# A two-layer decoder trunk on one core: sparse-attention probabilities times values as split products for four heads at once, more projections by halves of K, and a raw-weight ring of three

## The chip, the core and the metric

The kernel runs on one core of a Trainium2 chip. The core has five engines with queues of their own: TensorE (PE, with its weight loads shown as PEld), VectorE (DVE), ScalarE (ACT), GpSimd (POOL) and SyncE (SP, which issues the transfers). The metric is the device time of one execution in microseconds (us), the median of several runs. Every time below is from the profile of one execution or from those runs.

## What is computed

A sequence of 512 tokens of width 1024 goes through two layers. Each layer normalises, projects, runs two groups of attention heads, multiplies each branch by a gate, projects back and adds; after that comes a gated per-layer embedding. The change touches mostly branch A of layer 0, a sparse attention in which each query keeps its best 128 causal keys by an indexer's score. Eight query heads share one key and one value head of 64 columns:

```python
def _dsa_attention(q, k, v, q_idx, k_idx, w_idx):      # cut
    ...
    score = jnp.where(causal[None], score, -jnp.inf)
    _, sel = lax.top_k(score, top_k)
    ...
    kg = k[bidx, sel]
    vg = v[bidx, sel]
    s = jnp.einsum('bqhd,bqkd->bqhk', qb, kg) * scale
    pr = jax.nn.softmax(s, axis=-1).astype(v.dtype)
    return jnp.einsum('bqhk,bqkd->bqhd', pr, vg)

def _even_layer(...):                                  # cut
    oa = _dsa_attention(aq, ak, av, iq, ik, iw)
    ob = _sliding_window_sink_attention(bq, bk, bv, b_sinks)
    ya = oa.reshape(bsz, seq, A_WIDTH) * jax.nn.silu(ag)
    yb = ob.reshape(bsz, seq, B_WIDTH) * jax.nn.silu(bg)
    return jnp.concatenate([ya, yb], axis=-1) @ w_out
```

Layer 1 has the branches C (dilated attention) and D (differential attention) in the same frame.

## The kernel before

Tokens are worked in four tiles of 128 (`NT`), the model width in eight pieces of 128 (`NK`). A product that has to be exact to float32 is made of split operands: `hilo` (line 337) writes a value's rounded part with ScalarE (`hi`) and the remainder with VectorE (`lo`), both in the reduced float32 format, and `PASSES` (line 381) multiplies hi by hi, hi by lo and lo by hi, three matmuls of 512 columns. Weights come in through `load_w` (line 346) into a ring of four tiles `raw` of 128x512, are split into a ring of eight tiles `w2`, and are multiplied by the split activations `AT`.

`proj_tok` (line 388) has three orders. "kt" runs over the K pieces outside and the four output banks `mm` inside, so that all four banks are complete at the end; "mix" does the first four K pieces so, and then, one bank after the other, the last four, handing each bank over as it is complete; "tok" does one bank after the other. `proj_gate` (line 443) makes a branch's gate and has one order, that of "kt".

Attention of A and B is `attend_four` (line 693): for one query tile `qb` and four heads, scores into the banks `sk`, then `exp_rows` (VectorE adds the mask and takes the row's extreme, ScalarE exponentiates), ScalarE scales by the reciprocal of the sum, and `probs_t` (line 633) turns the probabilities by TensorE transposes into the one bank `tk`, which ScalarE copies to `pt` in float32. Then one float32 matmul of 128 columns for each head and key block multiplies `pt` by the values `Ve` into the bank `ob`, and `put_y` writes the result to `Y`, by ScalarE, or by VectorE with the gate multiplied in where the gate is there already. C already does it the other way: `turned` (line 623) transposes up to four blocks, `hilo` splits them into `pt`, and matmuls with up to 512 columns multiply them by a value tile whose 128 columns are 64 of hi and 64 of lo; `add_halves` adds the two halves of the result.

The order of the instructions of all engines is not the order of the code. `Program` records every call, and `order` (line 211) lays them out by a list schedule: on each engine the ready call of lowest rank goes first, where a rank is the call's place in the code less a lead from the table `LEADS` (line 31). The orders are then fixed; each engine works its list from front to back. SyncE issues all weight loads and the moves of heads. All is in one function, and the trace gives every instruction the line of its outer caller (L260), so that the rows below are told apart by tile names.

Of the kernel before, what the change touches and what calls it, by code (L numbers as in the profile page):

```python
# [12 lines left out]
F32 = mybir.dt.float32  # L13
# [8 lines left out]
P = 128  # L22
# [9 lines left out]
    "att": (-47, 57, 0, 53, 0, 124, 103, 328, -453, -409, 0, 0, 65, 346, 15, -135, -12, -62, 201, 25, 64, -25, -77,  # L32
# [6 lines left out]
    "idx": (-5, 38, 12),  # L39
    "mm": (0, 71, -13, 0, 0, 8, -171, 58, -43, 0, 16, 1, 0, 0, -20, 0, -21, 212, 58, -17, 0, 42, 10, -107, 178, -10,  # L40
         -7, -2, 8, -2),
    "norm": (-1359, -2, 2, 0, 228, -8, -7, -723, -109, 136, 0, 728, -122, -190, 196, 14, 146, 1654, 86, -1, 1, 0,
         -277, -9),
    "rows": (-312, -61, 0, -98),
    "rs": (0, 0, 160),
    "ss": (121, 0, -149, -59, -2, 107, -255, -64, 1, 167, 231, 226, 0, -95, 298, 72, 0, 34, 18, 45, -118, -139, -39,
         0, -102, 85, 7, 30, -79, -161, 0, -49),
    "tab": (2592, 1756, 76, 2, -41, 0),
    "top": (0, -183, -691, -1133, 45, 7, 5, 0, 5, -296, -294, -351),
    "w": (0, 226, 357, 520, 348, 94, -40, 291, 8, -115, 15, 22, 54, -173, 0, 41, 45, 193, -113, -15, 99, 144, -123,  # L50
         59, 194, -22, -64, -41, -621, -1474),
    "x": (-445, -66),
    "y": (1366, 84, 36, 1, 1288, 252, 91, -16, 10, 0, 1032, 24, -46, -55, -384, -1003),
    None: 0,
# [5 lines left out]
PR = 8  # L60
SHORT = 400
# [202 lines left out]
def tile_trunk(ctx: ExitStack, tc: tile.TileContext, a: dict, out: bass.AP):  # L264
# [9 lines left out]
    def uid(s):  # L274
        cnt[0] += 1
        return f"{s}{cnt[0]}"
# [10 lines left out]
    def o_bank():  # L287
        return ps.tile([P, 512], F32, name=uid("ob"), tag="ob", bufs=1)
# [57 lines left out]
    def load_w(parts, kts):  # L346
        raws = []
        n = sum(w for _, w in parts)
        for kt in kts:
            raw = sb.tile([P, 512], F32, name=uid("raw"), tag="raw", bufs=4)  # L350
            o = 0
            for src, w in parts:
                nc.sync.dma_start(out=raw[:, o:o + w], in_=src[kt * P:(kt + 1) * P, :])
                o += w
            raws.append((kt, raw[:, :n]))
        return raws, n
# [86 lines left out]
    def proj_gate(pieces_n, y0, done, rsb, swap=0):  # L443
# [3 lines left out]
        for i, (kt, w2) in enumerate(pieces):  # L447
            for m in range(4):
                for c, (xa, wa) in enumerate(PASSES):
                    nc.tensor.matmul(banks[m], w2[:, wa, m * P:(m + 1) * P], AT[:, xa, kt ^ (4 * swap), :],  # L450
                                     start=(i == 0 and c == 0), stop=(i == last and c == 2))
# [241 lines left out]
    def attend_four(qb, key0, qT, kv, g, V, mask, y0, sink=None):  # L693
# [130 lines left out]
    for k0, k1 in ((1, 2), (2, 3), (3, 4)):  # L824
        load_xT(k0, k1)
        wiq[0].extend(load_w(ecols("iq"), range(k0, k1))[0])
# [116 lines left out]
    proj_tok(wbq, head_evac(bqT, (tab_bq[:, 0], tab_bq[:, 1]), rs0, put=put_stacked))  # L943
# [5 lines left out]
    proj_tok(waq, head_evac(aqT, (tab_aq[:, 0], tab_aq[:, 1]), rs0, put=put_stacked))  # L949
# [55 lines left out]
    proj_tok(weights(ocols("cv"), range(NK), 2), cv_evac, swap=1)  # L1005
# [83 lines left out]
    proj_tok(wcq, head_evac(cqT, (tab_cq[:, 0], tab_cq[:, 1]), rs1, put=put_far), swap=1)  # L1089
# [5 lines left out]
    proj_tok(weights(ocols("dv"), range(NK), 2), dv_evac, swap=1)  # L1095
# [4 lines left out]
    proj_tok(wdk, head_evac(dkT, (tab_dk[:, 0], tab_dk[:, 1]), rs1, put=put_stacked), swap=1)  # L1100
    wdq = weights(ocols("dq"), range(NK), 2)
    dqT = {}
    proj_tok(wdq, head_evac(dqT, (tab_dq[:, 0], tab_dq[:, 1]), rs1, put=put_far), swap=1)
# [68 lines left out]
```

## Time and profile before

| | us |
|---|---|
| median of three runs | 664.13 (663.04 to 664.13) |
| the profiled execution | 663.99 |
| its span, from first to last instruction | 662.1 |
| TensorE busy | 655.2 |
| VectorE busy | 531.9 |
| ScalarE busy | 415.9 |

The span is 1.9 us shorter than the time of the same execution; the rest lies around it. The page gives each engine's busy time, the span in 40 slices of 16.6 us with a digit for each (tenths of the slice that the engine was busy), the chain of work that ended last, and groups of instructions by tile. A busy TensorE means that matmuls are in its pipe, not that it starts one at every chance; how fast they follow each other is read from how many fit in a stretch.

### The profile page before, as it was taken

How to read it: one execution, taken by the hardware profiler on the slowest of the kernel's cores; microseconds unless marked ns; L12 is line 12 of the kernel's file. 1: busy time of each engine (PE TensorE's matmuls, PEld its weight loads, DVE VectorE, ACT ScalarE, POOL GpSimd, SP SyncE). 2: the span in 40 equal slices, each digit the busy share in tenths (PEclk: the TensorE clock that was granted, in tenths of full speed). 3: DMA queues.
4: the chain of work that ended last, by engine and by line, in shares of the span. 5: the costliest groups of instructions: out<-in, count | busy, mean ns of one | idle time of the engine just before them, and what ended most of it. 6: DMA issues, size and time to landing. Idle time of an engine off the chain costs nothing.

```text
span 662.1 us, 10348 instructions
## 1 busy us (share of the span) xinstructions
PE 655.2 (99%) x3373; PEld 542.4 (82%) x3373; DVE 531.9 (80%) x1246; ACT 415.9 (63%) x937; POOL 66.3 (10%) x46
## 2 busy tenths in 40 slices
PE   9999999999999999999999999999999999999997
PEld 5888788889888888888878888888887878888886
DVE  6798999999999656786796297788697899768565
ACT  6675659989799933654564254776654586655431
POOL 0121133010000000000031041000053100000000
PEclk9999999999999999999999999999999999999999
DMA  8945155546111530542545438621286672323411
GB/s 329 341 134 144 49 147 156 160 132 219 33 57 43 189 96 16 175 144 94 161 141 148 125 120 257 196 81 49 74 244 175 213 224 66 121 61 98 127 65 64
DMA packets 76711, 90.50 MB, mean 137 GB/s; under 512 B 6640, under 2 KB 43888, under 8 KB 76400
## 3 DMA queue, kind: packets, MB, share of 16 engines
q1 hardware_dynamic: 76512, 89.81, 44.5%
q8 instruction: 27, 0.44, 0.3%
q14 instruction: 28, 0.23, 0.1%
q10 hardware_dynamic: 144, 0.02, 0.0%
HBM read 69.36 MB, written 10.49 MB: 121 GB/s over the span
## 4 chain that ended last, share of the span: by engine, by line
PE 90%; DMA 4%; DVE 3%; SPq 1%; issue 1%; ACT 1%; POOL 0%; POOLq 0%
PE mm L260 69%; PE ob L260 8%; PE tk L260 7%; PE sk L260 7%; DMA far<-ql 2%; DVE t L260 1%; SPq L260 1%; DMA raw<-in_w_in_odd_dram 1%; DMA raw<-in_w_in_even_dram 1%; DMA slot<-far 1%; DVE w L260 1%; DVE tiny L260 1%; DMA q<-far 0%; POOL tiny L260 0%; ACT w L260 0%
## 5 line engine op out<-in xcount | busy, mean ns | idle before, releaser
L260 PE MATMUL mm<-AT,w 128*128 128x512 f32 (+1 forms) x1176 | 293.9, 394 | 0.0
L260 PEld LDWEIGHTS mm<-AT,w 128*128 128x128 f32 x1176 | 211.6, 188 | 40.0 <-ACT raww L260 0.3
L260 PE MATMUL mm<-w,AT 128*128 128x512 f32 (+1 forms) x936 | 237.8, 398 | 0.3 <-DVE w L260 0.2
L260 PEld LDWEIGHTS mm<-w,AT 128*128 128x128 f32 x936 | 170.7, 188 | 34.8 <-DVE w L260 0.5
L260 ACT ACTIVATE w<-raw,gains 128x512 fp32r<-128x512 f32 x96 | 67.8, 723 | 55.8 <-PE mm L260 42.2
L260 DVE SCALAR_TENSOR_TENSOR w<-raw,gains,w 128x512 fp32r<-128x512 f32 x96 | 70.7, 746 | 34.0 <-ACT w L260 33.7
L260 POOL TENSOR_TENSOR tiny<-tiny,mhalf 128x8 f32<-128x8 f32 (+1 forms) x32 | 59.2, 1851 | 303.0 <-DVE tiny L260 290.6
L260 ACT ACTIVATE pr<-pr,nm 128x256 f32<-128x256 f32 (+3 forms) x128 | 69.1, 543 | 13.7 <-DVE nm L260 13.2
L260 DVE TENSOR_TENSOR w<-raw,w 128x512 fp32r<-128x512 f32 x80 | 53.5, 681 | 6.6 <-ACT w L260 6.1
L260 ACT CAST w<-raw 128x512 fp32r<-128x512 f32 x79 | 48.2, 625 | 15.7 <-PE mm L260 10.6
L260 PE MATMUL sk<-slot,slot 128*128 128x256 f32 (+3 forms) x248 | 56.5, 319 | 0.6 <-issue 0.3
L260 PEld LDWEIGHTS sk<-slot,slot 128*128 128x128 f32 x248 | 40.7, 189 | 8.2 <-ACT t L260 1.7
L260 PE MATMUL tk<-ident,pr 128*128 128x128 f32 x256 | 44.1, 274 | 0.1
L260 PEld LDWEIGHTS ob<-pt,Ve 128*128 128x128 f32 x272 | 36.7, 191 | 4.2 <-ACT pt L260 1.9
L260 PE MATMUL ob<-pt,Ve 128*128 128x128 f32 x272 | 39.4, 276 | 0.0
L260 ACT ACTIVATE t<-t 128x512 f32<-128x512 f32 (+1 forms) x33 | 20.2, 618 | 30.1 <-DVE t L260 30.1
L260 ACT COPY pt<-tk 128x512 f32<-128x512 f32 (+3 forms) x56 | 27.6, 493 | 17.4 <-PE tk L260 14.0
L260 DVE CUSTOM_DVE_ANT_0 pr<-sk,cpack 128x128 f32<-128x128 f32 (+3 forms) x72 | 31.3, 460 | 7.5 <-PE tk L260 3.7
L260 PEld LDWEIGHTS tk<-ident,pr 128*128 128x128 f32 x256 | 31.2, 140 | 6.4 <-ACT pt L260 1.3
L260 DVE TENSOR_TENSOR t<-mm,rows 128x512 f32<-128x512 f32 (+1 forms) x33 | 21.8, 669 | 17.4 <-PE mm L260 12.1
L260 DVE TENSOR_TENSOR slot<-slot,mm 128x512 f32<-128x512 f32 x32 | 21.3, 683 | 17.5 <-PE mm L260 17.4
L260 ACT CAST AT<-slot 128x512 fp32r<-128x512 f32 x40 | 24.2, 616 | 16.8 <-PE mm L260 8.7
(112 smaller groups left out, 791.5 us busy)
## 6 DMA issues: line engine op xcount, KB each, us to landing
raw<-in_w_in_odd_dram SPq DMA_DIRECT2D x64, 256.0 KB, 3.0
raw<-in_w_in_even_dram SPq DMA_DIRECT2D x36, 256.0 KB, 3.4
raw<-in_w_ple_gate_dram SPq DMA_DIRECT2D x32, 256.0 KB, 3.1
slot<-qh SPq DMA_DIRECT2D x38, 128.0 KB, 2.7
slot<-ql SPq DMA_DIRECT2D x38, 128.0 KB, 2.5
slot<-far SPq DMA_DIRECT2D x36, 128.0 KB, 3.3
raw<-in_w_out_even_dram SPq DMA_DIRECT2D x16, 256.0 KB, 2.9
raw<-in_w_out_odd_dram SPq DMA_DIRECT2D x16, 256.0 KB, 3.1
```

The source lines that it names most:

```text
L260: getattr(getattr(nc, engine), method)(*args, **kw)
```

## The change

1. **A's products.** For all query tiles (`WIDE = 0`) of branch A, four heads' blocks of one key block are transposed together by `turned`, so the probabilities are split into hi and lo, and two matmuls of 512 columns replace four float32 matmuls of 128 columns. The value tile `V2` holds hi and lo columns side by side, scaled by a half through `rsh`, and is written in `small_evac`. The two halves of the result are added: a copy by ScalarE and an add by VectorE, and a multiplication more where the gate is there already.
2. **By halves of K.** `proj_tok` gets "mix" for bq, aq, cv, cq, dv, dk and dq; `proj_gate` always works like "mix".
3. **Ring.** `raw` has three tiles instead of four; the place of the fourth is `V2`'s, which one early weight tile uses first.
4. **Leads.** The whole table `LEADS` has other numbers, so that the order of all engines is another.

```diff
 LEADS = {
-    "att": (-47, 57, 0, 53, 0, 124, 103, 328, -453, -409, 0, 0, 65, 346, 15, -135, -12, -62, 201, 25, 64, -25, -77,
+    "att": (15, 42, -531, -131, 82, 0, 8, 0, 230, 105, -283, 0, 0, 0, 59, 94, -251, -240, -154, -5, 0, 3, 10, 0, 0,
...
+WIDE = 0
...
-    def load_w(parts, kts):
+    def load_w(parts, kts, tag="raw"):
...
-            raw = sb.tile([P, 512], F32, name=uid("raw"), tag="raw", bufs=4)
+            raw = sb.tile([P, 512], F32, name=uid("raw"), tag=tag, bufs=1 if tag == "V2" else 3)
...
-        for i, (kt, w2) in enumerate(pieces):
-            for m in range(4):
-                for c, (xa, wa) in enumerate(PASSES):
+        for i, m in [(i, m) for i in range(4) for m in range(4)] + [(i, m) for m in range(4) for i in range(4, last + 1)]:
+            kt, w2 = pieces[i]
+            for c, (xa, wa) in enumerate(PASSES):
...
         ob = o_bank()
+        if qb >= WIDE and sink is None:
+            for kb in range(nkb):
+                pt = turned([pr[:, kb * P:(kb + 1) * P] for pr in prs])
+                for c in range(2):
+                    nc.tensor.matmul(ob, V2[:, kb].rearrange("p u d -> p (u d)"), pt[:, c], start=kb + c == 0,
+                                     stop=kb == nkb - 1 and c == 1)
+            halves = ob.rearrange("p (k j n) -> p k j n", k=2, j=2)
+            for j in range(2):
+                ys = Y[y0][64 * j:64 * j + 64, 2 * g:2 * g + 2, qb * P:(qb + 1) * P]
+                both = [halves[64 * u:64 * u + 64, :, j, :] for u in range(2)]
+                if gated.get(y0):
+                    z = tmp()[64 * j:64 * j + 64, :256].rearrange("p (k n) -> p k n", k=2)
+                    nc.scalar.copy(out=z, in_=both[0])
+                    nc.vector.tensor_tensor(out=z, in0=z, in1=both[1], op=ALU.add)
+                    nc.vector.tensor_tensor(out=ys, in0=z, in1=ys, op=ALU.mult)
+                else:
+                    nc.scalar.copy(out=ys, in_=both[0])
+                    nc.vector.tensor_tensor(out=ys, in0=ys, in1=both[1], op=ALU.add)
+            return
...
+    V2 = sb.tile([P, NT, 2, HD], F32R, name="V2", tag="V2", bufs=1)
+    rsh = const.tile([P, NT], F32, name="rsh")
...
     def small_evac(t, bank):
+        nc.vector.tensor_scalar(out=rsh[:, t:t + 1], in0=rs0[:, t:t + 1], scalar1=0.5, scalar2=None, op0=ALU.mult)
...
+        hilo(V2[:, t, 0, :], V2[:, t, 1, :], bank[:, 256:320], rsh[:, t:t + 1])
...
-    proj_tok(wbq, head_evac(bqT, (tab_bq[:, 0], tab_bq[:, 1]), rs0, put=put_stacked))
+    proj_tok(wbq, head_evac(bqT, (tab_bq[:, 0], tab_bq[:, 1]), rs0, put=put_stacked), order="mix")
```

The instruction orders show the change at three places. TensorE, the third and fourth key block of A's last product group (`ob694` before, `ob688` after; `mm` rows between are the output projection), before:

```order
L260 MATMUL tk701_781<-ident_69,pr693_773 128x128
L260 MATMUL mm727_807<-AT_73,w2722_802 128x512 x2
L260 MATMUL ob694_774<-pt700_780,Ve_147 128x128
L260 MATMUL mm728_808<-AT_73,w2722_802 128x512
L260 MATMUL ob694_774<-pt700_780,Ve_147 128x128
L260 MATMUL mm728_808<-AT_73,w2722_802 128x512
L260 MATMUL ob694_774<-pt700_780,Ve_147 128x128
```

The same place on TensorE after:

```order
L261 MATMUL ob688_770<-pt694_776,V2_148 128x512
L261 MATMUL tk695_777<-ident_69,pr682_764 128x128
L261 MATMUL tk695_777<-ident_69,pr683_765 128x128
L261 MATMUL tk695_777<-ident_69,pr686_768 128x128
L261 MATMUL tk695_777<-ident_69,pr687_769 128x128
L261 MATMUL mm733_815<-AT_73,w2726_808 128x512
L261 MATMUL mm724_806<-AT_73,w2720_802 128x512
L261 MATMUL mm734_816<-AT_73,w2726_808 128x512
L261 MATMUL mm733_815<-AT_73,w2726_808 128x512
L261 MATMUL ob688_770<-pt696_778,V2_148 128x512
```

One product of 512 columns and its twin stand for four of 128, and between a block's transposes and its products stand fewer rows of other work.

VectorE after the last exponent of A (`slot703`, `slot699`, `slot700` are the sums with the residual, `slot117` is `Y` of A, `w2` rows are weight splits), before:

```order
L260 TENSOR_TENSOR w2724_804<-raw723_803,w2724_804 128x512
L260 RECIPROCAL r685_765<-den684_764 128x4
L260 TENSOR_TENSOR w2742_822<-raw741_821,w2742_822 128x512
L260 SCALAR_TENSOR_TENSOR slot117_195<-ob674_754,slot117_195 64x2x128 x2
L260 TENSOR_TENSOR slot703_783<-slot703_783,mm713_793 128x512
L260 TENSOR_TENSOR slot703_783<-slot703_783,mm714_794 128x512
```

The same stretch of VectorE after:

```order
L261 TENSOR_TENSOR pt690_772<-tk689_771,pt690_772 128x512
L261 TENSOR_TENSOR slot700_782<-slot700_782,mm721_803 128x512
L261 TENSOR_TENSOR t675_757<-t675_757,ob666_748 64x256
L261 TENSOR_TENSOR t676_758<-t676_758,ob666_748 64x256
L261 TENSOR_TENSOR slot117_197<-t675_757,slot117_197 64x2x128
L261 TENSOR_TENSOR slot117_197<-t676_758,slot117_197 64x2x128
L261 TENSOR_TENSOR pt692_774<-tk691_773,pt692_774 128x512
```

The remainders `pt` of the probabilities, the adds of the halves and the gate's multiplications now stand in this queue among the other rows.

TensorE, the projection bq in the early part (`mm201` to `mm204` are its four banks), before:

```order
L260 MATMUL mm201_279<-w2134_212,AT_73 128x512 x3
L260 MATMUL mm202_280<-w2134_212,AT_73 128x512 x3
L260 MATMUL mm203_281<-w2134_212,AT_73 128x512 x3
L260 MATMUL mm204_282<-w2134_212,AT_73 128x512 x3
L260 MATMUL mm347_425<-w2246_324,AT_73 128x512 x3
```

The end of the first bank and the second bank of bq after:

```order
L261 MATMUL mm201_281<-w2132_212,AT_73 128x512 x3
L261 MATMUL mm201_281<-w2134_214,AT_73 128x512 x3
L261 MATMUL mm202_282<-w2128_208,AT_73 128x512 x3
L261 MATMUL mm202_282<-w2130_210,AT_73 128x512 x3
L261 MATMUL mm202_282<-w2132_212,AT_73 128x512 x3
```

The last four K pieces now go through one bank at a time, so the banks are complete one after the other.

## Rows read from the trace of the kernel before

**Rows 1.** Page: busy us, share, instructions; then the span in 40 slices
```profile
PE 655.2 (99%) x3373; PEld 542.4 (82%) x3373; DVE 531.9 (80%) x1246; ACT 415.9 (63%) x937; POOL 66.3 (10%) x46
...
DVE  6798999999999656786796297788697899768565
```

**Rows 2.** Chain that ended last, merged: start us, us, engine, tile, count
```profile
132.82 0.89 PE ob L260 x8
...
275.85 51.35 PE mm L260 x223
```

**Rows 3.** TensorE's groups: shapes, count, busy us, mean ns, idle before
```profile
L260 PE MATMUL tk<-ident,pr 128*128 128x128 f32 x256 | 44.1, 274 | 0.1
L260 PE MATMUL ob<-pt,Ve 128*128 128x128 f32 x272 | 39.4, 276 | 0.0
```

**Rows 4.** Windows: stretch, us, busy of PE, PEld, DVE, ACT, POOL; clock, DMA, GB/s
```profile
0.00:20.00 20.00, 18.51 (x71) 12.70 (x72) 13.34 (x22) 13.16 (x22) 0.45 (x7) 1.00 0.92 338
20.00:60.00 40.00, 40.00 (x201) 34.57 (x199) 35.09 (x88) 25.82 (x63) 7.45 (x8) 1.00 0.71 214
60.00:96.40 36.40, 36.40 (x176) 29.03 (x175) 35.51 (x77) 22.62 (x44) 8.87 (x4) 1.00 0.34 90
96.40:218.30 121.90, 121.90 (x751) 106.03 (x749) 120.54 (x377) 110.50 (x305) 7.96 (x4) 1.00 0.40 118
218.30:246.90 28.60, 28.60 (x173) 24.53 (x172) 16.07 (x31) 17.08 (x34) 0.00 (x0) 1.00 0.41 136
```

**Rows 5.** VectorE's timeline at the end of A: start us, us, instructions, idle before
```profile
216.77 1.02 DVE L260 TENSOR_TENSOR slot<-slot,t 128x384 f32<-128x384 f32 x2
217.71 0.68 DVE L260 CUSTOM_DVE_ANT_0 pr<-sk,acc 128x512 f32<-128x512 f32 x1
...
226.93 1.88 DVE L260 TENSOR_TENSOR slot<-slot,mm 128x512 f32<-128x512 f32 x3
...
229.93 1.28 DVE L260 TENSOR_TENSOR w<-raw,w 128x512 fp32r<-128x512 f32 x2
236.06 0.69 DVE L260 TENSOR_TENSOR slot<-slot,mm 128x512 f32<-128x512 f32 x1 [4.84 <-PE mm L260]
...
246.22 0.68 DVE L260 TENSOR_TENSOR AT<-slot,AT 128x512 fp32r<-128x512 f32 x1
```

**Rows 6.** TensorE's timeline at A's last products
```profile
242.06 0.38 PE L260 MATMUL ob<-pt,Ve 128*128 128x128 f32 x2
242.20 0.48 PE L260 MATMUL mm<-AT,w 128*128 128x512 f32 x1
242.51 0.38 PE L260 MATMUL ob<-pt,Ve 128*128 128x128 f32 x2
242.65 12.61 PE L260 MATMUL mm<-AT,w 128*128 128x512 f32 x54
```

**Rows 7.** VectorE's groups like the added operations
```profile
L260 DVE TENSOR_TENSOR pt<-tk,pt 128x512 fp32r<-128x512 f32 x8 | 5.5, 690 | 0.2
L260 DVE SCALAR_TENSOR_TENSOR slot<-ob,slot 64x256 f32<-64x256 f32 x4 | 1.7, 422 | 1.2 <-PE ob L260 1.2
L260 DVE SCALAR_TENSOR_TENSOR tab<-cpack,vpack 128x128 f32<-128x128 f32 x12 | 3.3, 280 | 0.0
```

**Rows 8.** ScalarE's groups of the same kind
```profile
L260 ACT COPY pt<-tk 128x512 f32<-128x512 f32 x28 | 16.4, 584 | 10.9 <-PE tk L260 9.9 <-PE sk L260 0.7
...
L260 ACT COPY pt<-tk 128x384 f32<-128x384 f32 x12 | 5.8, 481 | 5.6 <-PE tk L260 3.3 <-PE ob L260 2.2
...
L260 ACT CAST pt<-tk 128x512 fp32r<-128x512 f32 x8 | 4.7, 583 | 0.1
```

**Rows 9.** TensorE's timeline where layer 1 waits for fetched heads
```profile
417.14 1.17 PE L260 MATMUL sk<-slot,slot 128*128 128x512 f32 x4 [0.27 <-DMA slot<-far]
```

**Rows 10.** DMA issues: tile, queue, count, KB each, median us to landing
```profile
raw<-in_w_in_odd_dram SPq DMA_DIRECT2D x64, 256.0 KB, 3.0
raw<-in_w_in_even_dram SPq DMA_DIRECT2D x36, 256.0 KB, 3.4
```

More of the change, by code (lines that the diff above doesn't have):

```diff
@@ L31 @@
 LEADS = {
-    "att": (-47, 57, 0, 53, 0, 124, 103, 328, -453, -409, 0, 0, 65, 346, 15, -135, -12, -62, 201, 25, 64, -25, -77,
[6 rows of a table removed]
[L39 to L54, printed above, removed]
+    "att": (15, 42, -531, -131, 82, 0, 8, 0, 230, 105, -283, 0, 0, 0, 59, 94, -251, -240, -154, -5, 0, 3, 10, 0, 0,
[6 rows of a table added]
+    "idx": (31, -130, 1),
+    "mm": (-4, -24, 57, -165, 0, -1, 298, 3, 0, -16, 11, -3, 5, 0, -37, 19, 0, 245, 20, 99, -95, 99, 14, -123, 4, 1,
+         0, -157, -115, -3166),
+    "norm": (-62, -691, 1, 0, 213, 2, -3177, 1551, 2183, 0, 108, 0, -1, 646, 70, -167, -914, 271, -191, -35, 699, -30,
+         -189, 1196),
+    "rows": (-272, -2, -443, -220),
+    "rs": (0, -143, -121),
+    "ss": (781, 0, 0, 0, 0, -1, -51, -137, 55, 1, 0, 0, 26, 1, -9, 2, -152, 1, -20, 0, 0, 0, -11, 0, -3, 288, -4, 250,
+         0, 0, 0, -16),
+    "tab": (-343, -27, 476, 3, 0, -62),
+    "top": (103, -148, -439, -910, 73, 49, -9, -20, 222, 0, -23, -373),
+    "w": (-68, 7, 0, 14, -51, -14, 2, -28, 22, -18, 0, -13, 0, -21, 0, -37, -129, 20, -41, 41, 146, -33, -61, 0, 89,
+         8, -97, -12, 60, 0),
+    "x": (-9, -91),
+    "y": (2183, 0, -51, -88, -41, 17, 845, 0, 1, -3, -47, 62, -187, -122, 168, 0),
+    None: 456,
 }
@@ L446, in proj_gate @@
         last = len(pieces) - 1
-        for i, (kt, w2) in enumerate(pieces):
-            for m in range(4):
-                for c, (xa, wa) in enumerate(PASSES):
-                    nc.tensor.matmul(banks[m], w2[:, wa, m * P:(m + 1) * P], AT[:, xa, kt ^ (4 * swap), :],
-                                     start=(i == 0 and c == 0), stop=(i == last and c == 2))
+        for i, m in [(i, m) for i in range(4) for m in range(4)] + [(i, m) for m in range(4) for i in range(4, last + 1)]:
+            kt, w2 = pieces[i]
+            for c, (xa, wa) in enumerate(PASSES):
+                nc.tensor.matmul(banks[m], w2[:, wa, m * P:(m + 1) * P], AT[:, xa, kt ^ (4 * swap), :],
+                                 start=(i == 0 and c == 0), stop=(i == last and c == 2))
         d = done * P
@@ L825, in tile_trunk @@
         load_xT(k0, k1)
-        wiq[0].extend(load_w(ecols("iq"), range(k0, k1))[0])
+        wiq[0].extend(load_w(ecols("iq"), range(k0, k1), "V2" if k0 == 3 else "raw")[0])
     for k0, k1 in ((0, 2), (2, 4)):
@@ L948, in tile_trunk @@
     aqT = heads()
-    proj_tok(waq, head_evac(aqT, (tab_aq[:, 0], tab_aq[:, 1]), rs0, put=put_stacked))
+    proj_tok(waq, head_evac(aqT, (tab_aq[:, 0], tab_aq[:, 1]), rs0, put=put_stacked), order="mix")
     pw0 = ple_products(0)
@@ L1003, in dv_evac @@
         nc.scalar.activation(out=dV[:, t, :], in_=bank, func=AF.Copy, scale=rs1[:, t:t + 1])
-    proj_tok(weights(ocols("cv"), range(NK), 2), cv_evac, swap=1)
+    proj_tok(weights(ocols("cv"), range(NK), 2), cv_evac, order="mix", swap=1)
     @nc.part("att")
@@ L1088, in tile_trunk @@
     fetched[1] = slot([P, 4, T], F32R)
-    proj_tok(wcq, head_evac(cqT, (tab_cq[:, 0], tab_cq[:, 1]), rs1, put=put_far), swap=1)
+    proj_tok(wcq, head_evac(cqT, (tab_cq[:, 0], tab_cq[:, 1]), rs1, put=put_far), order="mix", swap=1)
     wdg = weights(ocols("dg"), range(NK), 2)
@@ L1094, in tile_trunk @@
     dV = slot([P, NT, 512])
-    proj_tok(weights(ocols("dv"), range(NK), 2), dv_evac, swap=1)
+    proj_tok(weights(ocols("dv"), range(NK), 2), dv_evac, order="mix", swap=1)
     wdk = weights(ocols("dk"), range(NK), 2)
@@ L1099, in tile_trunk @@
     dkT = heads()
-    proj_tok(wdk, head_evac(dkT, (tab_dk[:, 0], tab_dk[:, 1]), rs1, put=put_stacked), swap=1)
+    proj_tok(wdk, head_evac(dkT, (tab_dk[:, 0], tab_dk[:, 1]), rs1, put=put_stacked), order="mix", swap=1)
     wdq = weights(ocols("dq"), range(NK), 2)
     dqT = {}
-    proj_tok(wdq, head_evac(dqT, (tab_dq[:, 0], tab_dq[:, 1]), rs1, put=put_far), swap=1)
+    proj_tok(wdq, head_evac(dqT, (tab_dq[:, 0], tab_dq[:, 1]), rs1, put=put_far), order="mix", swap=1)
     wcg = weights(ocols("cg"), range(NK), 2)
```

12 rows, old and new, of the table LEADS are left out of this document.

## Prediction, made before the changed kernel ran

> **What bounds the kernel now.** I read the page first, then the chain of waits, then windows cut at the events of branch A, and last the timelines of two engines at A's end. TensorE is busy for 655.2 of 662.1 us, VectorE for 531.9 [rows 1]. The busy share alone does not say that TensorE is at its pace, but the chain does: 223 matmuls of 512 columns in 51.35 us, 0.230 us each, and eight records of A's and B's float32 products in 0.89 us [rows 2]. So TensorE is the bound, and a us less of its work is a us of time as long as nothing else is late.
>
> Something else is nearly late. The slices of VectorE show nines from the fifth to the thirteenth [rows 1], and the windows make it exact: from 60 to 96.4 us it is busy for 35.51 of 36.40, and from there to the end of A's last exponent row (218.3) for 120.54 of 121.90 [rows 4]. Before 60 us it is idle for 6.66 and 4.91, then for 0.89 and 1.36: 13.8 us up to 218.3. From 218.3 to 246.9, the end of A's last split, it works 16.07 of 28.6 us [rows 4]; in one gap of 4.84 us it waits for TensorE's sums [rows 5]. These 12.5 us are the only reserve that VectorE has ahead of the output projection. The stretch is balanced: two engines full, the third (ScalarE, 110.5 of 121.9) not far from it.
>
> **The change part by part.** *A's products on TensorE.* A float32 product shows as two records: 272 of them [rows 3] are the 136 products of A (two groups, four heads, ten key blocks: 80) and B (56). Eight records in 0.89 us make 0.2225 us a product, 80 of them 17.8 us. After: two products of 512 columns for each of 20 key blocks, 40 x 0.230 = 9.2 us. The transposes stay 80. TensorE has 8.6 us less to do. If nothing else were late, that is 664.0 - 8.6 = 655.4 by the profiled execution's time.
>
> *What it costs VectorE.* Before, ScalarE alone took the turned probabilities out of the bank; now VectorE follows with the remainder. Its like is the 128x512 remainder of C at 0.690 us [rows 7]. But instructions overlap: three adds that follow each other take 1.88 us, so they start 0.60 apart, and of two splits the second starts 0.59 after the first [rows 5]. Twenty remainders cost 12.0 us. The halves of the result add, for three query tiles, 12 adds of 64x256, and for the last, whose gate is there already, 4 adds and 4 multiplications in the place of 4 multiplications: 16 more. The nearest row is 0.422 us [rows 7], less the same overlap of 0.08 gives 0.34, so 5.4 us (6.8 at the full 0.422). Eight short rows for V2 and rsh lie below the 0.28 of the 128x128 row [rows 7]; I take half of that, 1.1 us. In all 18.5 us.
>
> By the Trainium skill's page Perfetto Trace Analysis, section Optimizing Scalar/DVE Operations, a VectorE access to PSUM costs about 125 ns against 60 on SBUF. The rows show no such difference: the three adds above read PSUM and the splits read SBUF, and both start 0.6 us apart [rows 5]. By the page the twenty remainders would be an estimated 1.3 us longer, and the forecast below as much later; by the rows they are not.
>
> *What it costs ScalarE.* Before, A needed eight copies of 128x384, twelve of 128x512 and four shorter ones, 3.8 + 7.0 us and a little; after, twenty casts of 0.583, 11.7 us [rows 8]. The same work.
>
> *Where this lies.* The order of VectorE tells how much of its new work stands ahead of the last exponent of A: 12 remainders (7.2), 10 half sums (3.4) and the short rows (1.1); later than before stand one weight split, four gate steps of 128x384 at 0.51 (half of the 1.02 us in [rows 5]), one of 128x128 and some table rows, together about 4.2. Net 7.5 us, so that with the same idle time the last exponent ends at 218.3 + 7.5 = 225.8. From there to the remainder of A's last block its list has 24 rows of 512 columns (14.4), six of 384 (3.1), six of 64x256 (2.0) and seven short ones (about 1.3): 20.8 us, if it never waits. That is 246.6. Before, no product needed VectorE after the exponents, and this list had only to be through for the splits.
>
> TensorE's list up to A's last product loses the 8.6 us and takes in 15 matmuls of the output projection (3.5), so it could be there at 242.5 [rows 6] - 5.1 = 237.4. It must wait there, in all, for up to 9.2 us, spread over the twenty blocks. Behind it, from 242.7 to the end at 662.1, stand 419.4 us, now without those 15 matmuls: 415.9.
>
> The result depends on VectorE's idle time. Fully kept (13.8): 246.6 + 0.3 + 415.9 = 662.8 of span, 664.7 of time. It can't fall under the 6.66 of the start, where data are still coming [rows 4]; of the 4.91 between 20 and 60 us some should go, since bq is handed over bank by bank and the adds of the index scores no longer wait for all of it. I take 1.7 off, a third; for the range, from nothing to 4.
>
> *Halves of K.* No TensorE work is added or removed. In layer 1 the heads of cq and dq go out to memory and back; TensorE waits 0.27 us for that [rows 9], and its list is thin around it. Earlier banks can remove such waits, and they can bunch the evacuations and the need for weights: all eight weight tiles are wanted after half of the projection. Bounds: a gain of 2 us, a loss of 1; I take a gain of 1.
>
> *Ring of three.* A weight load can start when the tile three before (formerly four) is split. It lands in 3.0 to 3.4 us [rows 10], and a K piece lasts TensorE 12 x 0.230 = 2.8 us. Three tiles in a cycle of about 5 us (landing, ScalarE 0.6, VectorE 0.6, semaphores) still give one per 1.7 us, so it is free where ScalarE and VectorE are prompt. In VectorE's full stretch the new order puts over 4.7 us of its other rows between a split and the one three before in all but two cases. The count of loads on SyncE's queue stays, and the moves of heads stand between them as before; a load that waits for its tile holds up those moves too. Zero; up to 2 us if these and the later ones miss.
>
> **Forecast.** VectorE becomes the bound from the first A blocks to the end of A and gives back most of what TensorE saves: 246.6 - 1.7 + 0.3 + 415.9 - 1.0 = 660.1 of span, 662.0 of time. The profiled execution (663.99) and the median (664.13) differ by 0.14, so I give 662.0 for the median.
>
> **The rivals.** *TensorE stays the bound.* VectorE's waits before A shrink, or its order lets A's remainders come early enough that other matmuls cover them; then 655.4, with the gain in layer 1 654.4. For it: the 12.5 us of idle time in A's tail [rows 4]. Against: 18.5 us of work come in, the tail's own list is 20.8 us long, and 13.8 us of idle time are already counted as kept.
>
> *VectorE takes it all.* It keeps its idle time and layer 1 gives nothing: 664.7, no change that can be measured. For it: after 60 us it had only 2.3 us of idle time [rows 4], and the waits before come from the start.
>
> *The transposition bank.* There is one bank `tk`. Before, it came free after ScalarE's copy of 0.58; now VectorE's remainder must have read it too, 0.60 later at the least, and VectorE works its list in order. TensorE's next transposes, of any branch, and all that stands behind them wait. If each of the 20 blocks puts these 0.60 on TensorE's path, 655.4 + 12.0 = 667.4, slower. It decides when VectorE comes to the remainder more than about 1 us late: the next block's transposes stand some 3 us of TensorE work behind, the least cycle (transposes 0.4, copy, remainder, hops) is some 2.2. For it: VectorE has no slack there, and the pieces between are short (single matmuls). Against: the same late rows are already in the forecast, and the two waits overlap.
>
> **How the numbers follow.** The forecast's own range is 659.7 to 664.7 (idle time 4 less with layer 1's gain of 1, or neither); chance 0.45. TensorE stays the bound 0.17 (655 to 658), VectorE takes it all 0.18 (664 to 665.5), the bank or late weights 0.20 (665.5 to 669). Two runs of this kernel can tell 0.2%, 1.3 us, from no change: faster is below 662.8, slower above 665.5. Of the forecast's share about 0.33 lies below 662.8 and 0.12 above it. Faster 0.17 + 0.33 = 0.50; same 0.12 + 0.16 = 0.28; slower 0.20 + 0.02 = 0.22. The range that leaves out 2 in 10 goes from 656.5 to 667.0.
>
> **What would show it.** TensorE's group of A's products should be 40 records at 0.23 us by the chain; VectorE's busy time should be some 18 us above 531.9, all of it ahead of 260 us, with its window to A's last product as full as [rows 4] and the gap of 4.84 us gone. TensorE should show more than before of short waits in front of A's products or of transposes, and A's last product should come at 243 to 247, not at 238. If it comes at 238, the first rival holds; if at 250 or later, the third. Behind it, the time to the end should be 414 to 417 us. The forecast would be wrong in its base if the remainders followed each other at other than 0.60 us, or if the late weights stopped VectorE.

## The result and the profile after

The changed kernel takes 667.75 us (median of six runs, 666.85 to 669.77), the kernel before 663.25 beside it: a ratio of 1.0066, 95% interval 1.0057 to 1.0076. It is slower by 0.7%; the forecast was 662.0, faster. The profiled execution took 667.28 us, its span 665.4.

The page of the changed kernel, where [rows 1] stood for the one before (busy time and share of each engine, and VectorE's tenths in 40 slices):

```profile
PE 653.4 (98%) x3253; PEld 533.3 (80%) x3253; DVE 550.9 (83%) x1290; ACT 418.3 (63%) x941; POOL 64.5 (10%) x46
...
DVE  6799999999999999577695586687998889657665
```

VectorE has 19.0 us more to do (forecast 18.5), and TensorE's time is shorter by 1.8 us only. Of the 272 records of [rows 3] the 112 of B are left, and A's 160 are now 40 products (TensorE's groups, tiles of one shape: count, busy us, mean ns of one, idle time before):

```profile
L261 PE MATMUL ob<-pt,V 128*128 128x512 f32 x40 | 16.2, 413 | 0.0
L261 PE MATMUL ob<-pt,Ve 128*128 128x128 f32 x112 | 15.7, 280 | 0.6 <-ACT pt L261 0.5
```

A's end by VectorE's timeline (start, duration), for [rows 5]: the last exponent row ends at 222.3, and the list from there to A's last remainder has hardly a gap. The half sums (64x256) start 0.45 us before the row that follows them.

```profile
221.60 0.68 DVE L261 CUSTOM_DVE_ANT_0 pr<-sk,acc 128x512 f32<-128x512 f32 x1
...
222.33 0.42 DVE L261 TENSOR_TENSOR slot<-slot,ob 64x256 f32<-64x256 f32 x1
222.78 1.29 DVE L261 TENSOR_TENSOR slot<-slot,mm 128x512 f32<-128x512 f32 x2
...
240.78 0.69 DVE L261 TENSOR_TENSOR pt<-tk,pt 128x512 fp32r<-128x512 f32 x1
...
243.18 0.69 DVE L261 TENSOR_TENSOR pt<-tk,pt 128x512 fp32r<-128x512 f32 x1
```

TensorE's timeline there, for [rows 6]: A's last product ends at 244.57.

```profile
243.23 0.41 PE L261 MATMUL ob<-pt,V 128*128 128x512 f32 x1
243.47 0.86 PE L261 MATMUL mm<-AT,w 128*128 128x512 f32 x3
244.18 0.39 PE L261 MATMUL ob<-pt,V 128*128 128x512 f32 x1
```

The windows (for [rows 4]; length, then busy time of TensorE, its weight loads, VectorE, ScalarE and GpSimd), one of the kernel before and three of after:

```profile
100.00:140.00 40.00, 40.00 (x248) 34.54 (x247) 39.84 (x128) 38.45 (x109) 7.96 (x4) 1.00 0.57 161
```

```profile
20.00:60.00 40.00, 40.00 (x205) 34.00 (x204) 36.91 (x97) 28.06 (x71) 11.05 (x8) 1.00 0.66 192
...
100.00:140.00 40.00, 37.76 (x212) 30.32 (x212) 39.62 (x137) 34.96 (x103) 2.74 (x3) 1.00 0.48 133
...
220.00:245.00 25.00, 25.00 (x124) 19.56 (x123) 24.74 (x52) 19.03 (x40) 0.00 (x0) 1.00 0.46 158
```

So up to A's end, at 244.57 where 243 to 247 was forecast, things went about as written. Behind it stand 420.8 us to the end of the span (665.4); the forecast had 414 to 417. The loss lies there, in stages whose products the change did not touch. One stretch says where to look. In the last output projection 54 matmuls with the same operands follow each other without a break in both kernels (TensorE's timeline; before, then after):

```profile
617.20 12.63 PE L260 MATMUL mm<-AT,w 128*128 128x512 f32 x54
```

```profile
619.08 12.84 PE L261 MATMUL mm<-AT,w 128*128 128x512 f32 x54
```

The same work takes 0.21 us longer, 4 ns for each matmul, at a granted clock of 1.00 in both. There are 1128 such products, in which AT is the operand that moves through the array and a weight tile the one that rests in it: 1128 x 4 ns = 4.5 us, as much as the whole loss.

### The profile page after: what moved, and what is told of

It is laid out like the page before. It is cut to its first block, busy times and chain, and to the rows that moved or that the text cites. A ratio compares the mean times of both kernels' runs of the same rounds, so it can differ in the third digit from the quotient of the medians.

```text
span 665.4 us, 10111 instructions
## 1 busy us (share of the span) xinstructions
PE 653.4 (98%) x3253; PEld 533.3 (80%) x3253; DVE 550.9 (83%) x1290; ACT 418.3 (63%) x941; POOL 64.5 (10%) x46
## 4 chain that ended last, share of the span: by engine, by line
PE 82%; DVE 11%; ACT 3%; DMA 2%; issue 1%; SPq 0%; ACTq 0%; DVEq 0%
PE mm L261 65%; PE tk L261 6%; PE ob L261 6%; PE sk L261 5%; DVE t L261 3%; DVE few L261 2%; DVE pr L261 1%; DVE m L261 1%; ACT pr L261 1%; DMA raw<-in_w_in_odd_dram 1%; DVE w L261 1%; DVE ql L261 1%; DMA slot<-in_xT_dram 1%; DMA raw<-in_w_out_odd_dram 1%; DVE tiny L261 1%
## 5 line engine op out<-in xcount | busy, mean ns | idle before, releaser
L261 POOL TENSOR_TENSOR tiny<-tiny,mhalf 128x8 f32<-128x8 f32 (+1 forms) x32 | 56.3, 1762 | 317.8 <-DVE tiny L261 317.8
L261 DVE TENSOR_TENSOR t<-raww,tab 128x512 f32<-128x512 f32 x48 | 32.2, 687 | 5.4 <-ACT raww L261 5.2
L261 ACT CAST pt<-tk 128x512 fp32r<-128x512 f32 (+1 forms) x44 | 23.9, 543 | 18.8 <-PE tk L261 18.5
L261 ACT ACTIVATE raww<-mm,rsn 128x512 f32<-128x512 f32 (+1 forms) x31 | 20.3, 657 | 18.9 <-PE mm L261 14.4
L261 DVE TENSOR_TENSOR pt<-tk,pt 128x512 fp32r<-128x512 f32 (+1 forms) x44 | 28.1, 640 | 4.3 <-ACT pt L261 3.7
```

The source lines that it names most:

```text
L261: getattr(getattr(nc, engine), method)(*args, **kw)
```

## The experiments

**Where the tiles lie.** `rsh` is a small tile of its own, allocated ahead of the large pool. It takes 16 bytes of each partition, rounded up to 32, and everything allocated behind it lies 32 bytes higher: the first weight tile starts at byte 151072 and not at 151040 (the sum of the tiles ahead of it); AT, allocated earlier, stays at 27712. The theory: these 32 bytes are the 4 ns. The rival: the loss is in the new order of layer 1.

*a_place*: the changed kernel, same order, old addresses.

```diff
-    rsh = const.tile([P, NT], F32, name="rsh")
+    small = const.tile([P, NT + 2], F32, name="small")
+    rsh = small[:, :NT]
...
-    ld = const.tile([P, 2], F32, name="ld")
+    ld = small[:, NT:]
```

> The changed kernel with one difference: `rsh` takes four unused columns of the small tile `ld` instead of a tile of its own. The instructions and their order stay as they are; only SBUF addresses move: everything that is allocated behind `rsh` (the weight tiles `w2` among it) lies 32 bytes lower, at the byte addresses of the kernel before. Theory 'address': in the trace of the changed kernel 54 matmuls of the last output projection take 12.84 us against 12.63 before, 4 ns more each, and all 1128 products with a weight tile resting and AT moving show it; the address of the resting tile sets it, so it goes back to 12.63, the time falls by 1128 x 4 ns = 4.5 us, to about 663, no difference to the kernel before. Theory 'order': the loss comes from the new order of layer 1, from the halves of K or the ring of three; the 4 ns are the effect of what the other engines do; the time stays at 667.8 and the stretch at 12.84.

Measured: 663.68 us, 1.0013 times before (1.0001 to 1.0025). The stretch is back:

```profile
617.66 12.62 PE L261 MATMUL mm<-AT,w 128*128 128x512 f32 x54
```

*b_move32, b_move64*: the kernel before with `ld` allocated wider; all that lies behind it moves up.

```diff
-    ld = const.tile([P, 2], F32, name="ld")
+    ld = const.tile([P, 10], F32, name="ld")[:, :2]
```

> The kernel before with one difference: the small tile `ld` is made wider by unused columns, so that all that is allocated behind it lies 32 bytes higher, as in the changed kernel. Instructions and order are the same. Theory 'address': the stretch of 54 matmuls of the last output projection takes 12.84 instead of 12.63 us, and the time rises by some 4.5 us to about 668. Theory 'order': nothing changes, 663.3.

Measured: 666.56 us, 1.0059 (1.0042 to 1.0077): the address shift alone brings the loss, without the change.

```profile
618.88 12.85 PE L260 MATMUL mm<-AT,w 128*128 128x512 f32 x54
```

> The kernel before with everything behind `ld` 64 bytes higher. Theory 'address': it tells how coarse the grid is. If a resting tile that starts on a multiple of 64 bytes is enough, the time stays at 663.3 and 54 matmuls of the last output projection at 12.63 us; if it must be 128 or more, it is 668 and 12.84 as with 32 bytes. Theory 'order': 663.3.

(18 columns in the place of 10.) Measured: 661.12 us, 0.9974 (0.9964 to 0.9984), faster than before, which neither theory said. In the table below both kinds of products are faster.

*b_at0, b_at128, b_at192*: the kernel before with AT allocated earlier, so that AT gets another address and the weight tiles stay. The edit below is b_at0's; b_at128 puts AT alone ahead, b_at192 `sink` and AT. The small tiles behind them move up too; the table further down goes by products of AT and weight tiles alone.

```diff
+    gains = const.tile([P, 4, NK], F32, name="gains")
+    AT = const.tile([P, 2, NK, T], F32R, name="AT")
     cpack = const.tile([P, CPACK], F32, name="cpack")
...
-    gains = const.tile([P, 4, NK], F32, name="gains")
...
-    AT = const.tile([P, 2, NK, T], F32R, name="AT")
```

> The kernel before with `gains` and `AT` allocated first: AT then starts on a multiple of 256 bytes (before: 64 above one), the weight tiles stay where they are. The 936 products of the token projections have AT resting and a weight tile moving; they take 0.233 us each in both kernels, the 1128 others took 0.229 before. Theory 'address', if the resting operand decides: the 936 go to 0.229 too, the time falls by some 3.5 to 4 us to 659.5, faster than before. If the two operands' addresses have to differ in some way, the 1128 get slower and the time rises instead, to 667. Theory 'order': 663.3.

Measured: 660.15 us, 0.9965 (0.9954 to 0.9977).

> The kernel before with AT allocated first: it starts 128 bytes above a multiple of 256, the weight tiles on one. So far, with the distance from the weight tiles to AT in bytes: 0 gives 0.2284 us a matmul whichever operand moves; 64 gives 0.2296 with AT moving and 0.2330 with a weight tile moving; 32 gives 0.2330 for both. Theory 'distance to the next multiple of 128': as 0, and 660. Theory 'of 256': it may be anything, and 662 to 668 if 0 is the only good distance.

Measured: 665.21 us, 1.0037 (1.0027 to 1.0048).

> The kernel before with `sink` and AT allocated first: AT starts 192 bytes above a multiple of 256. Theory 'distance, to a multiple of 128': as 64, so as the kernel before in both kinds, 663. Theory 'distance with its sign, moving less resting, to a multiple of 256': the two kinds change places, AT moving 0.2330 and a weight tile moving 0.2296: 1128 x 3.4 ns more and some 840 x 3.4 ns less, 664.

Measured: 664.64 us, 1.0024 (1.0014 to 1.0033); the two kinds change places, as the theory of the signed distance said. Two stretches of b_at192, one for each kind; the kernel before has 12.62 (a weight tile moving, x53) and 12.63 (AT moving, x54):

```profile
347.94 12.39 PE L260 MATMUL mm<-w,AT 128*128 128x512 f32 x53
...
617.19 12.85 PE L260 MATMUL mm<-AT,w 128*128 128x512 f32 x54
```

The mean distance between the starts of two such matmuls in a row (some 920 pairs of the one kind, 670 of the other, pairs over 250 ns left out), by the distance in bytes from the weight tiles up to AT:

| run | distance, modulo 256 | AT moving, ns | weight tile moving, ns | us against before |
|---|---|---|---|---|
| b_at0 | 0 | 228.2 | 228.4 | -2.7 |
| b_move64 | 0 | 228.3 | 228.5 | -1.8 |
| before | 64 | 229.6 | 233.0 | |
| a_place | 64 | 229.7 | 233.2 | +0.8 |
| changed kernel | 32 | 233.1 | 233.1 | +4.5 |
| b_move32 | 32 | 233.1 | 233.0 | +3.7 |
| b_at128 | 128 | 232.4 | 232.3 | +2.1 |
| b_at192 | 192 | 233.3 | 229.8 | +1.5 |

For the products with a weight tile moving, the distance from the resting to the moving operand is the table's taken from 256. Read by moving less resting operand, the two columns agree: 0 gives 228.2 to 228.5, 64 gives 229.6 to 229.8, 128 gives 232.3 to 232.4, and 32, 192 and 224 give 233.0 to 233.3. Neither operand's own address does it, and a distance of 128 is not as good as 0. Modulo 512 the distance is 256 in b_at0 (AT at 16640) and 0 in b_move64 (first weight tile at 151104), and the paces are the same to 0.1 ns; so 256 is the step as far as these runs go. The times follow: for b_at128, 1128 x 2.8 ns - 840 x 0.7 ns = 2.6 us, measured 2.1; for b_at192, 1128 x 3.7 - 840 x 3.2 = 1.5, measured 1.5; for b_move32, 1128 x 3.5 = 3.9, measured 3.7. Only the gains come short: at distance 0, 1128 x 1.3 + 840 x 4.6 ns = 5.3 us would be had, and 2.7 and 1.8 arrive (the intervals of these two overlap, so that they can't be told apart). A part is lost up to A's end, where VectorE is nearly full: in b_at0's trace A's last product ends at 242.42, 0.5 us earlier than before, where 280 x 1.3 + 264 x 4.6 ns = 1.6 us would be had. The rest is open.

**What A's products are worth.** Three runs on a_place, with all other instructions in the same order. *a_nolo* leaves the remainders out, and the second product reads the rounded part again. *a_bankfree* keeps the remainders' work but takes it off the bank: they subtract the rounded part from itself. So both leave out the low part of A's probabilities. *a_olda* takes A's products back to four float32 products from one copied block; the remainders, V2 and the sums of halves go with them (the edit shown is that of the products).

```diff
                 pt = turned([pr[:, kb * P:(kb + 1) * P] for pr in prs])
+                nc.instead[len(nc.calls) - 1] = []
                 for c in range(2):
+                    nc.instead[len(nc.calls)] = [("matmul", (ob, V2[:, kb].rearrange("p u d -> p (u d)"), pt[:, 0]), dict(
+                        start=kb + c == 0, stop=kb == nkb - 1 and c == 1))]
```

> On a_place (the changed kernel with its weight tiles back at the old addresses, 663.7 us). The 20 remainder rows of A's turned probabilities are not issued, and the second product of each key block reads the rounded part again: A's result lacks the low part, VectorE has 20 x 0.60 = 12 us less to do, TensorE the same, all else stands in the same order. Theory 'VectorE eats it' and theory 'the transposition bank' expect the same here: TensorE gets its 8.6 us, 656 to 658.5. If A's stage is not what holds the time (theory 'layer 1 eats it'), it stays within 1.5 us of 663.7.

Measured: 662.35 us. Two theories expected 5 to 8 us less than a_place; it is 1.3 less by the medians and 0.9 by the ratios (1.0000, 0.9988 to 1.0011, and 1.0013), which the noise of the two runs can't tell from nothing. The third theory expected such a time, but its reason isn't borne out: A's stage still decides when A's last product comes. In the second and third window VectorE is now idle for 4.45 and 4.22 us (a_place: 0.28 and 0.26), and A's last product ends only 1.0 us earlier (a_nolo, then a_place):

```profile
242.62 0.39 PE L262 MATMUL ob<-pt,V 128*128 128x512 f32 x1
```

```profile
243.63 0.39 PE L261 MATMUL ob<-pt,V 128*128 128x512 f32 x1
```

Between 100 and 140 us TensorE is idle for 2.07 us (a_place: 2.28), nearly as long as with the remainders, while VectorE is full with rows that are not A's remainders.

```profile
100.00:140.00 40.00, 37.93 (x214) 30.46 (x213) 39.30 (x135) 35.32 (x102) 3.02 (x3) 1.00 0.46 135
180.00:220.00 40.00, 40.00 (x206) 33.05 (x205) 35.55 (x94) 34.47 (x83) 0.00 (x0) 1.00 0.19 60
220.00:245.00 25.00, 25.00 (x126) 20.19 (x124) 20.78 (x43) 18.56 (x38) 0.00 (x0) 1.00 0.48 171
```

```diff
+                hi = pt[:, 0].bitcast(F32)
+                nc.instead[len(nc.calls) - 1] = [("tensor_tensor", (), dict(out=pt[:, 1], in0=hi, in1=hi, op=ALU.subtract))]
                 for c in range(2):
```

> On a_place, same order. The 20 remainder rows of A subtract the rounded part from itself in place of the bank `tk` (so the low part is zero): VectorE's work is the same, but the bank comes free after ScalarE's copy, some 0.7 us or more earlier. Theory 'the transposition bank': the time falls about as far as without the remainders, to 656 to 658.5. Theory 'VectorE eats it': no change, 663 to 664.

Measured: 665.53 us, 1.0041 (1.0027 to 1.0054). Nothing is gained, so the bank isn't what holds TensorE. That it is 1.8 us slower than a_place wasn't explained. VectorE's remainders in a_place (20 of A, 8 of C), then A's 20 in a_bankfree, by count, busy us and mean ns:

```profile
L261 DVE TENSOR_TENSOR pt<-tk,pt 128x512 fp32r<-128x512 f32 x28 | 19.3, 688 | 0.6 <-ACT pt L261 0.3
```

```profile
L262 DVE TENSOR_TENSOR pt<-pt 128x512 fp32r<-128x512 f32 x20 | 13.7, 687 | 0.5 <-ACT pt L262 0.3
```

```diff
+                nc.instead[at - 2] = [("copy", (), dict(out=pt[:, 0].bitcast(F32), in_=nc.calls[at - 2][1][0][2]["in_"]))]
+                nc.instead[at - 1] = []
                 for c in range(2):
+                    nc.instead[at + c] = [("matmul", (ob[:, h * P:(h + 1) * P], Ve[:, (V(key0 + kb) - h % 2) * HD:
+                                           (V(key0 + kb) - h % 2 + 2) * HD], pt[:, 0, h * P:(h + 1) * P].bitcast(F32)),
+                                           dict(start=kb + h == 0, stop=kb == nkb - 1 and h == 3)) for h in (2 * c, 2 * c + 1)]
```

> a_place, same order of instructions, with A's products as in the kernel before: each turned block is copied once in float32, no remainder, four float32 products of 128 columns in the place of two of 512, no sums of halves, V2 not written. TensorE has 8.6 us more to do, VectorE 18 us less. Theory 'the split products are worth something although both engines are full': slower than a_place by 2 to 6 us, 666 to 670. Theory 'VectorE eats all of it': the same or faster, 661 to 664.

Measured: 668.87 us, 1.0104 (1.0083 to 1.0124), 5.2 more than a_place. A's last product now ends at 251.14, 7.1 later:

```profile
249.32 0.67 PE L262 MATMUL ob<-pt,Ve 128*128 128x128 f32 x4
250.53 0.61 PE L262 MATMUL ob<-pt,Ve 128*128 128x128 f32 x4
```

So in the new order the split products are worth 5.2 us net of what they cost VectorE, more than half of TensorE's 8.6. But the new order with the old products is 6.2 us slower than the kernel before.

**The stop at 509 us.** In a_place TensorE stands for 1.9 us in the gate of C, in the changed kernel for 1.7 us, 2 us later in the run. a_place's timeline, all engines (SPq is SyncE's queue; in brackets the idle time and what ended it):

```profile
503.12 2.71 SPq L261 DMA_DIRECT2D slot<-ql  x2
...
504.71 0.69 DVE L261 TENSOR_TENSOR ql<-tk,qh 128x512 fp32r<-128x512 f32 x1
...
505.93 0.55 SPq L261 DMA_DIRECT2D raw<-in_w_in_odd_dram  x1
...
509.47 0.72 ACT L261 ACTIVATE w<-raw,gains 128x512 fp32r<-128x512 f32 x1 [4.26 <-DMA raw<-in_w_in_odd_dram]
510.10 0.67 ACT L261 ACTIVATE raww<-mm,rsn 128x512 f32<-128x512 f32 x1
...
510.82 2.72 PE L261 MATMUL mm<-AT,w 128*128 128x512 f32 x6 [1.86 <-ACT raww L261]
```

Read from below: TensorE waits for a bank, which ScalarE empties (`raww`); that copy stands behind a weight split that waits for its load; the load stands on SyncE's queue behind a move of heads, which waits for VectorE's remainder `ql`. And then the clock (a_place's windows; the figure behind the five busy times, 0.66 in the second row, is TensorE's granted clock):

```profile
505.00:510.00 5.00, 3.96 (x18) 2.91 (x16) 3.48 (x7) 0.74 (x2) 1.94 (x1) 1.00 0.69 178
510.00:515.00 5.00, 4.18 (x13) 3.42 (x14) 3.16 (x5) 2.58 (x6) 0.00 (x0) 0.66 0.48 172
```

For a part of the second stretch the clock was at the lower of its two levels, 1.2 and not 2.4 GHz, right behind the stop. This is one execution, of 665.16 us; the median of a_place is 663.68.

*a_ring4* gives layer 1 a ring of four in V2's place, planned anew.

```diff
+            loads[0] += loads[1]
+            tag_ = tag or ("V2" if loads[1] and loads[0] % 4 == 0 else "raw")
-            raw = sb.tile([P, 512], F32, name=uid("raw"), tag=tag, bufs=1 if tag == "V2" else 3)
+            raw = sb.tile([P, 512], F32, name=uid("raw"), tag=tag_, bufs=1 if tag_ == "V2" else 3)
```

> On a_place. From layer 1 on every fourth raw weight tile uses the place of `V2`, which A's end leaves free, so that the ring there has four tiles as in the kernel before; the order is planned anew. In a_place a weight piece of dq was asked for at 505.9 us, landed at 509.4, ScalarE waited 4.3 us for it with the evacuation of a bank behind it, and TensorE stood for 2.0 us; the granted clock of the next 5 us was 0.66 there. Theory 'the ring of three': this wait goes, and the time falls by 2 to 4 us, to 660 to 661.7, with runs that scatter less than the 662.2 to 665.2 of a_place. If the loads are late only because of the moves of heads ahead of them on SyncE's queue: 663 to 664.

(The piece is the gate's, not dq's.) Measured: 664.11 us, 1.0022 (1.0011 to 1.0032). The wait goes, and the new plan brings others, 1.5 us for heads from memory and 1.4 for a VectorE row, so that the run decides nothing. *a_ring4s* keeps the order of a_place:

> As a_ring4 (from layer 1 on every fourth raw weight tile uses the place of V2), but laid out by the plan for a ring of three, so that the instructions stand in the same order as in a_place and the ring of four only lets a load start earlier. In a_ring4 the new plan itself brought other waits of 1.6 and 1.8 us. Theory 'the ring of three': the stop of 2.0 us at 508.6 goes, and with it the fall of the granted clock in some executions; 660.5 to 662, with less scatter. Theory 'the moves ahead of it': the load still stands behind them, 663 to 664.

Measured: 671.52 us, 1.0126 (1.0108 to 1.0145). It was no clean test: the plan runs a few loads in another order than the code, so that two tiles in V2's place stood two loads apart. TensorE's waits (total, times, longest) show new ones, the first of 4.8 us:

```profile
PE ob L265 <- ACT pt L265: 5.3, 3, 4.8
PE mm L265 <- ACT raww L265: 2.0, 1, 2.0
```

*a_ring4c* gives V2's place to every fourth load of the planned order, *a_ring4f* also puts the one load ahead of the four moves:

```diff
+            for i in self.early:
+                moves = [k for k in order[:order.index(i)] if self.calls[k][0] == "sync"][-4:]
+                order.remove(i)
+                order.insert(order.index(moves[0]), i)
```

> As a_ring4s, same order as a_place, but V2's place goes to every fourth load in the order in which the plan runs them, so that each tile is free once the tile four before is split. The piece that TensorE stood for at 508.6 us in a_place is the last of the gate of C (the text of a_ring4 says dq). Theory 'the ring of three': it is asked for earlier than 505.9, the stop goes, 660.5 to 662. Theory 'the moves ahead of it': it still stands behind four moves of heads, the last of which waits for VectorE's remainder that ends at 505.4; no change, 663 to 664.

Measured: 663.23 us, 1.0010 (1.0001 to 1.0020). The load is asked for at 504.95, and the stop is 1.2 us.

```profile
502.88 2.03 SPq L266 DMA_DIRECT2D slot<-ql  x2
504.95 0.60 SPq L266 DMA_DIRECT2D raw<-in_w_in_odd_dram  x1
```

> a_ring4c with this one load put ahead of the four moves of heads on SyncE's queue; nothing else moves. It can be asked for at about 501.8 instead of 505.9 us and lands at about 505.3, before ScalarE comes to it. Both theories expect that the stop of 2.0 us goes, with the falls of the clock behind it: 660.5 to 662. If the time stays at 663 to 664, something else would have come late at that place.

Measured: 662.30 us, 0.9993 (0.9984 to 1.0003); the stop is gone, the clock is 1.00 there, and the load is asked for 7.5 us earlier than in a_place:

```profile
498.41 0.60 SPq L271 DMA_DIRECT2D raw<-in_w_in_odd_dram  x1
```

So the stop costs 1.4 us in all by the medians, 1.3 by the ratios. How ring and moves share it isn't shown: a_ring4c's time can't be told from a_place's (the intervals overlap, though its stop is 0.7 us shorter), and the load ahead of the moves wasn't run with a ring of three.

**The halves of K.** *a_l1kt* undoes "mix" in layer 1 and in the gates.

```diff
-    proj_tok(weights(ocols("cv"), range(NK), 2), cv_evac, order="mix", swap=1)
+    proj_tok(weights(ocols("cv"), range(NK), 2), cv_evac, swap=1)
```

> On a_place. In layer 1 the projections cv, cq, dv, dk and dq and all gates go back to K outside, the four banks inside (bq and aq stay by halves, since the table of leads has no plan without them); the order is planned anew by the same table. Theory 'the halves of K cost' (all eight weight tiles are wanted at half of the projection, banks are evacuated in a bunch): the time falls by 1 to 3 us, to 661 to 662.5. The forecast's term (halves of K gain 1): it rises to 664.5 or more. The table was made for the other order, which may add to either.

Measured: 677.33 us, 1.0214 (1.0196 to 1.0233). Table and code were planned for each other, so this doesn't tell what the halves are worth. The table of before gives no order for the new code, nor the new table one for the old code, and so the halves weren't tried apart from the leads; that stays open.

**A version that beats both.** *a_place_at0* is a_place with AT as in b_at0; *a_best* is a_ring4f with it.

> a_place with `gains` and `AT` allocated first, as in b_at0, so that AT and the weight tiles both start on multiples of 256 bytes. b_at0 gained 2.7 us on the kernel before, its matmuls of 512 columns at 0.2284 us where the kernel before has 0.2296 (AT moving) and 0.2330 (a weight tile moving). Theory 'address': both kinds go to 0.2284 here too, and the time falls by 2 to 4.5 us, to 659.5 to 661.5. Where VectorE sets the pace, up to A's end, a faster TensorE gives nothing, which is why it may be less than 1128 x 1.2 + 690 x 4.6 ns = 4.5 us.

Measured: 661.08 us, 0.9966 (0.9955 to 0.9976).

> a_ring4f with AT and the weight tiles both on multiples of 256 bytes, as in a_place_at0 (661.1). If the stop is worth 1.5 to 2 us, 659 to 659.8, faster than b_at0 (660.15); without it 661.

Measured: 658.41 us, 0.9932 (0.9916 to 0.9949), a little better than expected: 0.7% faster than the kernel before, and 1.7 us ahead of b_at0 (0.9954 to 0.9977).

## Why the prediction was wrong

**The change part by part: a part was missing.** The forecast took `rsh` for some short rows of VectorE. It is also a tile, and the shift that it brings made 1128 matmuls 3.5 to 4 ns longer each: 667.75 - 663.68 = 4.1 us by the medians, 3.5 by the ratios (1.0066 less 1.0013), 3.7 in b_move32. No term and no rival had it: where the tiles lie was put at nothing, without a reason. With the old addresses the time, 663.68 in a_place, lies within the forecast's own range. The prediction also carried the 0.230 us of a matmul in the kernel before over to the changed one, where it is 0.233.

**TensorE's term held.** The 40 products came as forecast. Without the remainders on either side, A's last product comes at 251.14 with the old products (a_olda) and at 243.01 with the new ones (a_nolo): 8.1 us, for 8.6 forecast.

**VectorE's term held, its place in part by luck.** Its work grew by 19.0 us for 18.5, the gap of 4.84 us of [rows 5] is gone, and between 20 and 60 us its idle time fell from 4.91 to 3.09 us, 1.8 for the 1.7 forecast. The last exponent ends at 222.3, 1.8 us ahead of the forecast (225.8 less 1.7). The list behind it then took 1.2 us more than forecast, 0.7 of it because the six rows of 64x256 take 0.45 us each and not 0.34. So A's last product comes at 244.57, near the forecast of 246.6 - 1.7 + 0.3 = 245.2, since two errors nearly cancel.

**The place of the waits was wrong.** TensorE alone was to be at A's last product at 237.4, with up to 9.2 us of waits spread over the twenty blocks. With the remainders gone (a_nolo) it comes at 243.0. The waits lie earlier: 40.00 - 37.76 = 2.24 us idle between 100 and 140 us, where before none was; A's first split product starts only at 132 us. The idle time shows less than half of it, since a matmul counts as busy for some 0.4 us while the next one can start after 0.23. Counted from start to start, against the usual distance of each kind of product in the traces, TensorE loses 5.6 us between 100 and 140 us in the changed kernel, 5.2 in a_nolo and 0.5 in the kernel before. That is most of the way from 237.4 to 243.0. VectorE is full there (39.62 of 40 us), but so it was before (39.84), and a_olda, with the old products and without VectorE's new work, loses 5.2 us there as well. So the waits come with the new order, not with the split products; which part of the order brings them wasn't tried. So *TensorE stays the bound* was out of reach in this order, and *VectorE takes it all* was too simple: both engines are full in turn, and relieving VectorE of the remainders brings A's last product 1.0 us forward.

**The transposition bank** is refuted: a_bankfree gains nothing, and the waits ahead of transposes that the changed kernel's trace lists come to 0.8 us, none on a remainder. In a_bankfree the 20 remainders read SBUF twice and not the bank: 687 ns each, against 688 with the bank (28 rows in a_place). The Trainium skill, page Perfetto Trace Analysis, section Optimizing Scalar/DVE Operations, gives a VectorE access about 60 ns on SBUF and 125 ns on PSUM, where the bank lies. At this width the rows don't show the difference, as the forecast chose to believe.

**Halves of K, a gain of 1.** It did not show in the one trace that can tell. In a_ring4f, with the old addresses and without the stop, 660.0 - 244.0 = 416.0 us stand behind A's last product: what the forecast had without that gain (415.9). Whether a gain is hidden there by another loss is open.

**Ring of three, 0 to 2.** Put at zero and mis-sized: the stop costs 1.4 us, with the falls of the clock. The moves of heads between the loads stood in the text, but with the cost on the moves, while here it was the load that waited.

Together, against the kernel before, forecast -2.1 and measured +4.5: 6.6 apart: 3.5 to 4.1 are the addresses, 1.4 the stop, 1 the gain that did not come, 5.9 to 6.5 in all. By absolute time a_ring4f, at 662.30, lands on the forecast of 662.0, but that is luck: the kernel before ran at 662.7 to 663.3 in the comparisons, not at the 664.13 from which the forecast started.

## What to carry to other kernels

A new tile, however small, moves every tile allocated behind it: when a matmul stream slows by a per cent or two with the same operands, compare equal stretches of it in both traces, and try the moving and the resting tiles at equal offsets modulo 256 bytes, the best of the six distances tried here. Where two engines are full, cost a change on both lists and look for waits ahead of the place that it touches: here TensorE lost 5.6 us there. On a queue worked in order, ask of each load what stands ahead of it and what that waits for.

## What the runs showed of the hardware

- The distance in time of two matmuls of 512 columns in the reduced float32 format depends on the SBUF addresses of the two operands: 228.2 to 233.3 ns, by moving less resting address modulo 256 (table above). The six distances tried are all that is known; the cause wasn't shown.
- A stop of TensorE of 1.86 us was followed by a stretch of 5 us at a mean granted clock of 0.66 in one execution (a_place), and by none below 1.00 in another with a stop of 1.74 us (the changed kernel).
- A VectorE remainder of 128x512 took 688 ns with one operand in PSUM (28 rows in a_place) and 687 ns with both in SBUF (20 rows in a_bankfree).
